# A feed-forward block in two stages: 2x2 block products for the up projection, a trip through DRAM, and a down projection by four feature tiles

## The chip, the cores and the metric

One core of one Trainium2 chip runs the whole program. Times are microseconds of device time for one execution. Of the kernel before, three runs are given; the profile is of one further execution.

## The reference

Two layers of a hybrid backbone over 1024 latent tokens of width 1024, with 256 context tokens beside them in layer 0 (layer 1 computes the latent tokens alone). Each layer is a modulated RMSNorm, an input projection into three head groups (latent attention, a state space scan, windowed attention), an output projection with a gated residual, and then the part that changes:

```python
def conv_glu(h, w_up, conv_w, conv_b, w_down):
    val, gate = jnp.split(h @ w_up, 2, axis=-1)
    return (jax.nn.silu(dwconv(gate, conv_w, conv_b)) * val) @ w_down

h2 = modulate(rms_norm(x, p['norm2_g']), sh2, sc2)
x = x + g2 * conv_glu(h2, p['ffn_w_up'], p['ffn_conv_w'], p['ffn_conv_b'], p['ffn_w_down'])
```

`w_up` is 1024 x 5632, so 2816 hidden features (22 tiles of 128) for the gate and 2816 for the value; `w_down` is 2816 x 1024. The convolution runs along the tokens with three taps. The modulation vectors (`mod`, twelve pieces of 512 columns per layer, each for the latent and for the context conditioning) are the product of a conditioning vector with `w_mod`.

## The kernel before

Activations lie with features on the partitions and tokens in the free dimension: eight tiles of 128 features for `x`, in token chunks of 512, 512 and (layer 0) 256. Every matrix product keeps nearly full fp32 precision by splitting both operands into a high and a low part and adding three products, so that one 128 x 128 weight tile against 512 tokens is three matmuls (`PASSES`, helper `mm` at L142):

```python
PASSES = ((0, 0), (0, 1), (1, 0))
```

A weight tile is fetched by SP (L410), cast to its high part by ACT (L420), and its low part is the difference on DVE (L421).

`ffn` walks over the 22 feature tiles. For each it makes the gate projection (24 matmuls per chunk of 512), whose result goes through bias and middle tap on ACT (L500), the two outer taps on DVE (L496) and SiLU on ACT (L508); then the value projection, whose result is multiplied into the gate by DVE (L1522), cast by ACT (L1523) and split by POOL (L1524). After every second tile, `do_down` adds what these two features give to all eight output tiles: six matmuls per output and chunk, and one DVE instruction that adds the result to `x` (L1501). So PE always has up and down products of the same stretch to run, and `x` stays in the on-chip memory.

The input of the block is prepared by `Norm`: DVE multiplies `x` by the inverse norm (L1911, L1917), ACT and DVE make high and low parts. `Norm` starts when the last outputs of the output projection `w_out` are there; the first gate product waits for it.

Modulation vectors are made by `mods_v` without PE's help: SP fetches two rows of blocks of `w_mod` (L344, 512 KB), DVE multiplies and adds (L349, L351), PE transposes 128 columns at a time into the tile `pt` (L147), and DVE sums (L358). It is a background generator: the program's planner gives it a turn after every `gap` of planned PE time. Six pieces of layer 0 run in the input projection of layer 0 (`early`), two more and all twelve of layer 1 in the FFN of layer 0.

SP issues all large transfers from one queue, in program order; each may wait for a semaphore, and what stands behind it waits with it.

## Time and profile before

| what | value |
|---|---|
| runs | 3346.91 us median of 3 (3344.35 to 3354.57) |
| the profiled execution | 3349.32 us, of which the span 3347.6 us |
| mean granted clock of TensorE | 0.967 of full speed |
| busy share: PE, DVE, ACT, POOL | 94%, 58%, 32%, 24% |
| FFN of layer 0 in the trace | about 902 to 1850 us |
| FFN of layer 1 in the trace | about 2588 to 3307 us |

The page and the views count an engine as busy while an instruction of it executes; matmuls are pipelined, so that their single durations overlap, and the rate of a stretch is its length over its count. The granted clock is the share of TensorE's full speed (2.4 GHz) that was allowed in a stretch; the lower level is 1.2 GHz.

### The profile page before, as it was taken

The page shows a single profiled execution, that of the slowest core. Times are in us where ns is not written, and L with a number is a line of the kernel's source. Part 1 is how long each engine was busy: PE and PEld are TensorE (multiplying, and loading weights), DVE is VectorE, ACT ScalarE, POOL GpSimd, SP SyncE. Part 2 cuts the span into 40 slices and gives each one's busy share as a digit, 9 for nine tenths or more (in the row PEclk, how much of TensorE's full clock was granted, in tenths as well). Part 3 has the DMA queues.
Part 4 walks back from the last instruction along what each step waited for, and adds up shares of the span by engine and source line. Part 5 has one row for each costly group of instructions (what it writes and reads, how often), then busy time and mean ns, then how long its engine had stood idle before and what let it go on. Part 6 is the DMA issues. An engine that isn't in the chain of part 4 may idle for free.

```text
span 3347.6 us, 40209 instructions
## 1 busy us (share of the span) xinstructions
PE 3160.3 (94%) x15857; PEld 2496.6 (75%) x15857; DVE 1948.8 (58%) x2912; ACT 1068.7 (32%) x1764; POOL 804.2 (24%) x518
## 2 busy tenths in 40 slices
PE   6999879989989999999999999879999999999998
PEld 4888645546878888888888788645558788888887
DVE  5966877664485565656544734886653544444444
ACT  5344543443331111111112533533342312212222
POOL 2115533452220000000001304553451200101102
PEclk9999879999999999999999999988999999999999
DMA  8765663103132222222111444843121111111111
GB/s 262 215 182 165 220 223 88 41 5 114 38 95 76 65 87 70 82 70 82 57 39 29 143 138 139 264 144 94 41 73 41 57 51 51 45 44 57 46 49 64
DMA packets 311550, 321.64 MB, mean 96 GB/s; under 512 B 34835, under 2 KB 250532, under 8 KB 311361
## 3 DMA queue, kind: packets, MB, share of 16 engines
q1 hardware_dynamic: 310396, 318.83, 31.1%
q8 instruction: 125, 2.05, 0.3%
q0 software_dynamic: 704, 0.14, 0.2%
q14 instruction: 65, 0.52, 0.0%
q10 hardware_dynamic: 260, 0.10, 0.0%
HBM read 249.09 MB, written 68.62 MB: 95 GB/s over the span
## 4 chain that ended last, share of the span: by engine, by line
PE 72%; DVE 8%; DMA 2%; issue 1%; ACT 1%; POOL 1%; SPq 0%; DVEq 0%; POOLq 0%; ACTq 0%
PE p L142 58%; PE s L142 5%; PE py L142 4%; DVE mx L1291 1%; DMA wm<-in_w_mod_dram 1%; DVE wm L351 1%; PE pm L142 1%; PE pn L142 1%; PE pd L142 1%; DVE acc L1326 1%; PE sb L142 0%; DMA ab<-acsd 0%; DVE sh L725 0%; DVE smx L1045 0%; PE pst L142 0%
## 5 line engine op out<-in xcount | busy, mean ns | idle before, releaser
L142 PE MATMUL p<-hhi,wh 128*128 128x512 f32 (+1 forms) x2552 | 943.8, 372 | 12.5 <-DVE ft L496 5.2
L142 PE MATMUL p<-hlo,wh 128*128 128x512 f32 (+2 forms) x2552 | 940.8, 369 | 7.4 <-POOL hlo L1920 6.6
L142 PE MATMUL p<-hhi,wl 128*128 128x512 f32 (+1 forms) x2504 | 923.6, 369 | 5.8 <-DVE wl L421 3.5
L142 PEld LDWEIGHTS p<-hhi,wh 128*128 128x128 f32 x2552 | 485.3, 190 | 95.6 <-issue 7.0
L142 PEld LDWEIGHTS p<-hlo,wh 128*128 128x128 f32 (+1 forms) x2552 | 483.2, 189 | 87.2 <-POOL hlo L1920 8.3
L142 PEld LDWEIGHTS p<-hhi,wl 128*128 128x128 f32 x2504 | 476.3, 190 | 87.2 <-DVE wl L421 5.6
L1524 POOL TENSOR_TENSOR gl<-ft,gh 128x512 fp32r<-128x512 f32 (+1 forms) x110 | 152.7, 1390 | 1404.6 <-ACT gh L1523 1404.6
L1501 DVE SCALAR_TENSOR_TENSOR x<-p,modT,x 128x512 f32<-128x512 f32 (+1 forms) x480 | 327.2, 695 | 240.2 <-PE p L142 239.8
L420 ACT CAST wh<-w 128x1024 fp32r<-128x1024 f32 (+2 forms) x188 | 193.2, 1040 | 751.4 <-PE p L142 706.3
L142 PE MATMUL p<-gh,wh 128*128 128x512 f32 (+1 forms) x880 | 325.7, 370 | 0.4 <-DVE x L1501 0.4
L142 PE MATMUL p<-gl,wh 128*128 128x512 f32 (+1 forms) x880 | 324.7, 369 | 0.0
L142 PE MATMUL p<-gh,wl 128*128 128x512 f32 (+1 forms) x880 | 323.9, 368 | 0.0
L421 DVE TENSOR_TENSOR wl<-w,wh 128x1024 fp32r<-128x1024 f32 (+1 forms) x181 | 224.9, 1252 | 146.5 <-ACT wh L420 145.3
L496 DVE SCALAR_TENSOR_TENSOR ft<-p,prm,ft 128x511 f32<-128x511 f32 (+2 forms) x264 | 157.8, 613 | 176.2 <-ACT ft L500 173.5
L351 DVE SCALAR_TENSOR_TENSOR wm<-wm,mstat,wm 128x512 f32<-128x512 f32 x280 | 202.6, 767 | 60.0 <-DMA wm<-in_w_mod_dram 59.9
L1375 ACT ACTIVATE P<-s 128x512 f32<-128x512 f32 x240 | 142.5, 598 | 247.0 <-PE s L142 240.8
L1522 DVE TENSOR_TENSOR ft<-ft,p 128x512 f32<-128x512 f32 (+1 forms) x110 | 69.4, 633 | 257.9 <-PE p L142 256.7
L1382 POOL TENSOR_TENSOR acc<-acc,P 128x1024 f32<-128x1024 f32 x69 | 169.5, 2456 | 185.1 <-ACT P L1375 162.3
L142 PEld LDWEIGHTS p<-gh,wh 128*128 128x128 f32 x880 | 165.9, 189 | 29.2 <-DVE x L1501 0.9
L142 PEld LDWEIGHTS p<-gh,wl 128*128 128x128 f32 x880 | 165.6, 188 | 28.2
L142 PEld LDWEIGHTS p<-gl,wh 128*128 128x128 f32 x880 | 166.0, 189 | 27.5 <-issue 0.2
L142 PE MATMUL py<-P,vt 128*64 128x512 f32 (+3 forms) x744 | 172.3, 578 | 0.0
(354 smaller groups left out, 4486.2 us busy)
## 6 DMA issues: line engine op xcount, KB each, us to landing
wm<-in_w_mod_dram SPq DMA_DIRECT2D x96, 512.0 KB
w<-in_ffn_w_up_dram SPq DMA_DIRECT2D x88, 512.0 KB
w<-in_ffn_w_down_dram SPq DMA_DIRECT2D x44, 512.0 KB
w<-in_w_in_dram SPq DMA_DIRECT2D x30, 512.0 KB
ab<-acsd SPq DMA_DIRECT2D x36, 384.0 KB
...
```

What stands on the lines that cost most here:

```text
L142: self.nc.tensor.matmul(out=out, lhsT=lhsT, rhs=rhs, start=start, stop=stop)
L351: nc.vector.scalar_tensor_tensor(out=acc[:, v, :], in0=w[:, i, :], scalar=c, in1=acc[:, v, :], op0=ALU.mult, op1=ALU.add)
L420: nc.scalar.copy(h, w)
L421: (nc.gpsimd if pool else nc.vector).tensor_sub(lo, w, h)
L496: nc.vector.scalar_tensor_tensor(out=dst[:, d0:d1], in0=src, scalar=w, in1=dst[:, d0:d1], op0=ALU.mult, op1=ALU.add)
L1291: nc.vector.tensor_reduce(out=m[:, j, s:s + 1], in_=p, axis=AXX, op=ALU.max)
L1326: nc.vector.reciprocal(rc, pd)
L1375: nc.scalar.activation(P[:, q * 512:(q + 1) * 512], s, AF.Exp, scale=sc)
L1382: (nc.vector if kt in ((2, 4, 6, 8) if self.scan else (4, 7)) else nc.gpsimd).tensor_add(acc, acc, P)
L1501: self.nc.vector.scalar_tensor_tensor(out=t[:, s:e], in0=p[:, 0:e - s], scalar=self.mcol(l, v, m)[:, o:o + 1], in1=t[:, s:e], op0=ALU.mult ...
L1522: nc.vector.tensor_mul(t[:, s:e], t[:, s:e], p[:, 0:e - s])
L1524: nc.gpsimd.tensor_sub(gl[:, s:e], t[:, s:e], gh[:, s:e])
```

## The change

The block becomes two stages per layer.

**Up.** A unit is a pair of neighbouring feature tiles of the gate or of the value (22 units: gate pair, value pair, gate pair, and so on). For the 1024 latent tokens a unit is a 2 x 2 block product: the weights in two column tiles by two halves of the depth (four 128-deep tiles each), the tokens in two halves of 512. Of the eight block products only seven are computed (with sums and differences of blocks ahead of and behind them). `UpNorm` makes the token blocks: 11, 12, 21, 22 as `Norm` did, then T1 to T4 as differences, in place in `x`, each split again into high and low parts. `up_weights` makes the weight blocks 11, 12, 22 and S1 to S4, and `wblock` splits each. `step` runs one product of 12 matmuls, and the results are added up in two tiles `cm` of the on-chip memory by DVE and ACT. `wrap` then does the convolution and SiLU, or the multiplication by the value, and writes the finished tile to DRAM (`gd`). Unit 0 is computed plainly; context tokens keep all their products.

**Down.** When all tiles are in DRAM, `gload` reads them back, ACT and DVE split them, and `down` takes four feature tiles at a time (two in the last group): 12 matmuls per output and chunk, then one addition to `x`. As `x` was used up for the blocks, `w_out` now also writes it to DRAM (`xsp`) and the down stage reads it again.

**Modulation.** Two pieces of layer 0 move from its FFN to `early` (eight pieces there, gap 3.0 for 4.0). Layer 1's twelve pieces move to the down stage of layer 0; eight of them are made for the latent conditioning alone (`nv`), and all must be done before the last group.

```diff
+GROUPS = [range(i, min(i + 4, NF)) for i in range(0, NF, 4)]
...
-    def mods_v(self, l, ns, wtile, gap, atile=None):
+    def mods_v(self, l, ns, wtile, gap, atile=None, nv=lambda n: 2):
...
-                    for v in range(2):
+                    for v in range(nv(n)):
...
+    def wblock(self, raw):
+
+        self.nblock += 1
+        t = self.W.tile([128, 2, *raw.shape[1:]], F32R, tag=("whi", "wlo")[self.nblock % 2], name=self.nm("wb"))
+        self.nc.scalar.copy(t[:, 0], raw)
+        self.nc.vector.tensor_sub(t[:, 1], raw, t[:, 0])
+        return t
...
+    def up_names(self, l, u):
+        return ("11", "12", "21", "22") if u == 0 else ("11", "12", "22", *(("21",) if l == 0 else ()), "S1", "S2", "S4", "S3")
...
+                if name == "S1":
+                    nc.vector.tensor_sub(a11, a11, a21)
+                    nc.vector.tensor_add(a21, a21, a22)
+                    raw = a21
+                elif name == "S2":
+                    nc.vector.tensor_sub(a22, a22, a11)
+                    raw = a22
+                elif name == "S4":
+                    nc.vector.tensor_sub(a12, a12, a22)
+                    raw = a12
+                else:
+                    raw = {"11": lambda: a11, "12": lambda: a12, "21": lambda: a21, "22": lambda: a22, "S3": lambda: a11}[name]()
+                w = self.wblock(raw)
+                if name == ("12" if u == 0 else "S4"):
+                    load(u + 1, 0)
+                if name == ("22" if u == 0 else "S3"):
+                    load(u + 1, 1)
...
+        def done(o, p, s, e):
+            self.resid(res[o], p, s, e, l, 2, o)
+            nc.sync.dma_start(out=self.spill[o][:, s:e], in_=res[o][:, s:e])
+            norm.feed(o, s, e)
...
+        def product(w, blk, psum, start, stop=True):
+            for k in range(4):
+                for i, (a, b) in enumerate(PASSES):
+                    self.mm(out=psum, lhsT=w[:, a, k, :], rhs=blk[k][b], start=(start and k == 0 and i == 0), stop=(stop and k == 3 and i == 2),
+                            skip_group_check=True)
+            self.tick()
...
+        def put(U_, j, half, p):
+            d = U_.cm[j][:, half * 512:(half + 1) * 512]
+            if (j, half) in U_.set:
+                nc.vector.tensor_add(d, d, p)
+            else:
+                nc.scalar.copy(d, p)
+            U_.set.add((j, half))
...
+            if s == "1":
+                U_.X = self.f("X")
+                product(weight(u, "11"), B["11"], U_.X, True)
+                put(U_, 0, 0, U_.X)
+            elif s == "2":
+                Y = self.f("Y")
+                product(weight(u, "12"), B["21"], Y, True)
+                put(U_, 0, 0, Y)
+            elif s == "4":
+                V = self.f("V")
+                product(weight(u, "22"), B["T4"], V, True)
+                put(U_, 1, 0, V)
+            elif s == "5":
+                U_.Z = self.f("Z")
+                product(weight(u, "S1"), B["T1"], U_.Z, True)
+                put(U_, 1, 1, U_.Z)
+            elif s == "6":
+                product(weight(u, "S2"), B["T2"], U_.X, False)
+                put(U_, 0, 1, U_.X)
+            elif s == "3":
+                product(weight(u, "S4"), B["22"], U_.Z, False)
+                put(U_, 0, 1, U_.Z)
+            elif s == "7":
+                product(weight(u, "S3"), B["T3"], U_.X, False)
+                out7(U_)
...
+        def wrap(u):
+
+            U_ = units.pop(u)
+            for j in range(2):
+                f = u // 2 * 2 + j
+                srcs = [(0, SEQ, U_.cm[j][:, LAT])] + ([(SEQ, NT, U_.pc[:, 256 * j:256 * j + 256])] if c else [])
+                if u % 2 == 0:
+                    t = gate[f] = self.u(name="ft")
+                    w0, w1, w2, b = conv_of(f)
+                    for s, e, p in srcs:
+                        nc.scalar.activation(t[:, s:e], p, AF.Identity, bias=b, scale=w1)
+                        for d0, d1, q, w in ((s + 1, e, p[:, 0:e - s - 1], w0), (s, e - 1, p[:, 1:e - s], w2)):
+                            nc.vector.scalar_tensor_tensor(out=t[:, d0:d1], in0=q, scalar=w, in1=t[:, d0:d1], op0=ALU.mult, op1=ALU.add)
+                    nc.scalar.activation(t[:, 0:n], t[:, 0:n], AF.Silu)
+                else:
+                    t = gate.pop(f)
+                    for s, e, p in srcs:
+                        nc.vector.tensor_mul(t[:, s:e], t[:, s:e], p)
+                    nc.sync.dma_start(out=self.gd[f][:, 0:n], in_=t[:, 0:n])
...
+        ps = plain(*chunks[0])
+        step(1, "1")
+        step(1, "2")
+        norm.need(chunks[1])
+        for j in range(2):
+            cv[j](ps[j], *chunks[0])
+        ps = plain(*chunks[1])
+        norm.built("T1")
+        if c:
+            norm.need(chunks[2])
+        for j in range(2):
+            cv[j](ps[j], *chunks[1])
+        if c:
+            for s in ("c11", "c12", "c21", "c22"):
+                step(0, s)
+        norm.built("T2")
+        norm.built("T3")
+        if c:
+            for j in range(2):
+                cv[j](units[0].pc[:, 256 * j:256 * j + 256], *chunks[2])
+            for s in ("c11", "c12", "c22", "c21"):
+                step(1, s)
+        norm.built("T4")
+        del units[0]
+        for s in ("5", "3", "6", "7", "4"):
+            step(1, s)
+        wrap(1)
+        for u in range(2, NF):
+            for s in ("1", "c11", "2", "c12", "4", "c22", "c21", "5", "6", "3", "7") if c else ("1", "2", "4", "5", "6", "3", "7"):
+                step(u, s)
+            wrap(u)
...
+        def gload(fs):
+            for f in fs:
+                t, h, lo = self.u(name="gr"), self.u(F32R, name="gh"), self.u(F32R, name="gl")
+                nc.sync.dma_start(out=t[:, 0:n], in_=self.gd[f][:, 0:n])
+                g[f] = h, lo
+                for s, e in chunks:
+                    nc.scalar.copy(h[:, s:e], t[:, s:e])
+                    nc.vector.tensor_sub(lo[:, s:e], t[:, s:e], h[:, s:e])
...
+        gload(GROUPS[0])
+        for o in range(KT):
+            t = self.X.tile([128, NT], F32, tag="x", name=self.nm("x"))
+            nc.sync.dma_start(out=t[:, 0:n], in_=self.spill[o][:, 0:n])
+            x.append(t)
+        start()
+        for i, fs in enumerate(GROUPS[:-1]):
+            for q in range(4):
+                ws = self.wnext(2, ahead=6)
+                for o in (2 * q, 2 * q + 1):
+                    for s, e in chunks:
+                        down(fs, ws, o, s, e)
+                if q == 0:
+                    gload(GROUPS[i + 1])
+            for f in fs:
+                del g[f]
+        before_last()
+        fs = GROUPS[-1]
+        ws = self.wnext(4, ahead=5)
+        for s, e in chunks:
+            for o in range(KT):
+                down(fs, [ws[o // 2]], o, s, e)
+                feed(o, s, e)
...
-            self.X = PoolTags(p, {"x": 8, "ft": 1, "wm": 2, "pn": 1} if l == 0 else {"x": 8, "ft": 1, "wm": 2})
+            self.X = PoolTags(p, {"x": 8, "ft": 1, "wm": 2, "pn": 1} if l == 0 else {"x": 9, "wm": 2})
...
-                        yield from self.mods_v(0, range(4, 10), wt, 4.0)
+                        yield from self.mods_v(0, range(4, 12), wt, 3.0)
...
+                    yield from self.mods_v(l + 1, range(12), xw, 4.6, xa, lambda n: 2 if n < 4 else 1)
...
+    def parts(self, name, k, raw, hi=None, lo=None):
+        nc = self.E.nc
+        if hi is None:
+            t = self.slot(name, k)
+            hi, lo = t[:, 0:512], t[:, 512:1024]
+        nc.scalar.copy(hi, raw)
+        nc.vector.tensor_sub(lo, raw, hi)
+        self.blk[name][k] = hi, lo
...
+            r = self.x[f][:, s:e]
+            hf, k = f // 4 + 1, f % 4
+            nc.vector.tensor_mul(r, r, pn[:, 0:e - s])
+            nc.scalar.activation(r, r, AF.Identity, bias=b[v][:, f:f + 1], scale=a[:, v, f:f + 1])
+            if v:
+                self.parts(f"c{hf}", k, r, self.slot(f"{hf}1", k)[:, SEQ:NT], self.slot("T1" if hf == 1 else "22", k)[:, SEQ:NT])
+            else:
+                self.parts(f"{hf}{1 if s == 0 else 2}", k, r)
...
+    def built(self, name):
+        nc = self.E.nc
+        for k in range(4):
+            t, u = self.x[k], self.x[4 + k]
+            c0, c1 = slice(*CHUNKS[0]), slice(*CHUNKS[1])
+            if name == "T1":
+                nc.vector.tensor_sub(t[:, c0], t[:, c1], t[:, c0])
+                self.parts(name, k, t[:, c0])
+            elif name == "T2":
+                nc.vector.tensor_sub(t[:, c1], u[:, c1], t[:, c1])
+                nc.vector.tensor_sub(u[:, c1], u[:, c1], t[:, c0])
+                self.parts(name, k, u[:, c1])
+            elif name == "T3":
+                self.parts(name, k, t[:, c1])
+            else:
+                nc.vector.tensor_sub(u[:, c0], u[:, c0], u[:, c1])
+                self.parts(name, k, u[:, c0])
```

`Norm` now feeds the blocks through `UpNorm.apply`. Lines of the changed program are shifted: its matmul helper is L143, its low parts of weights L437, of token blocks L2153.

**PE, a stretch of the up projection of layer 1.** Before, one output of 512 tokens is 24 matmuls into `p`:

```order
L142 MATMUL p_24083<-hhi_20121,wh_23945 128x512 [waits Activation_49]
L142 MATMUL p_24083<-hlo_20122,wh_23945 128x512
L142 MATMUL p_24083<-hhi_20121,wl_23946 128x512 [waits DVE_49]
L142 MATMUL p_24083<-hhi_20127,wh_23945 128x512
L142 MATMUL p_24083<-hlo_20128,wh_23945 128x512
L142 MATMUL p_24083<-hhi_20127,wl_23946 128x512
L142 MATMUL p_24083<-hhi_20134,wh_23945 128x512
```

Now a product is 12 matmuls, and some products go on in a bank that already holds another one (here `Z` of S1, `X` of S2 over `X`, then `Z` of S4 over `Z`):

```order
L143 MATMUL Z_20796<-hb_20437,wb_20695 128x512 [waits DVE_49,Activation_49]
L143 MATMUL Z_20796<-hb_20437,wb_20695 128x512 x2
L143 MATMUL Z_20796<-hb_20441,wb_20695 128x512 x3
L143 MATMUL Z_20796<-hb_20445,wb_20695 128x512 x3
L143 MATMUL Z_20796<-hb_20449,wb_20695 128x512 x3
L143 MATMUL X_20740<-hb_20466,wb_20712 128x512 [waits Activation_49]
L143 MATMUL X_20740<-hb_20466,wb_20712 128x512
L143 MATMUL X_20740<-hb_20466,wb_20712 128x512 [waits DVE_49]
L143 MATMUL X_20740<-hb_20471,wb_20712 128x512 x3
L143 MATMUL X_20740<-hb_20476,wb_20712 128x512 x3
L143 MATMUL X_20740<-hb_20481,wb_20712 128x512 x3
L143 MATMUL Z_20796<-hb_20360,wb_20742 128x512 [waits Activation_49]
```

Between the two visits to `Z` there is one product into `X`; `Z` is read out in between.

**SP, the end of the up projection of layer 0.** Before, the queue of the FFN holds weights (`w`) and pieces of `w_mod` (`wm`) in turn:

```order
L410 DMA w_12482<-in_ffn_w_up_dram 128x8x128 [waits DMAHW5_49,DVE_49]
L344 DMA wm_12426<-in_w_mod_dram 128x2x512 [waits DMAHW7_49,DVE_49]
L344 DMA wm_12535<-in_w_mod_dram 128x2x512 [waits DMAHW1_49,DVE_49]
L410 DMA w_12706<-in_ffn_w_up_dram 128x8x128 [waits DMAHW6_49,DVE_49]
L344 DMA wm_12643<-in_w_mod_dram 128x2x512 [waits DMAHW2_49,DVE_49]
L410 DMA w_12712<-in_ffn_w_up_dram 128x8x128 [waits DMAHW0_49,DVE_49]
```

Now the reload of `x`, the finished tiles (`gd<-ft`), the tiles read back (`gr`), down weights and pieces of `w_mod` stand in one line. The first group of the down stage needs four `gr`: the second, third and fourth are here, and the last two `x` wait for PE's last product:

```order
L1761 DMA x_11833<-xsp 128x1280 [waits DMAHW0_49,PE_49]
L1741 DMA gr_11791<-gd 128x1280 [waits DMAHW1_49,Pool_49]
L1761 DMA x_11835<-xsp 128x1280 [waits PE_49]
L1686 DMA gd<-ft_11581 128x1280 [waits DMAHW3_49,DVE_49]
L347 DMA wm_11867<-in_w_mod_dram 128x2x512 [waits DMAHW4_49,PE_49]
L613 DMA w_12103<-in_ffn_w_down_dram 128x4x256 [waits DMAHW6_49,DMAHW5_49,DVE_49]
L1686 DMA gd<-ft_11589 128x1280 [waits DVE_49]
L1741 DMA gr_11801<-gd 128x1280 [waits DMAHW7_49]
L347 DMA wm_11909<-in_w_mod_dram 128x2x512 [waits DMAHW0_49]
L347 DMA wm_11997<-in_w_mod_dram 128x2x512 [waits DMAHW4_49,DMAHW1_49,DVE_49]
L1741 DMA gr_11811<-gd 128x1280 [waits DMAHW2_49]
```

The fourth `gr` stands behind a `wm` that waits for DVE.

**DVE, the start of the FFN of layer 1.** Before, normalised tokens (`nt`) and their low parts (`hlo`):

```order
L1917 TENSOR_TENSOR nt_20310<-x_19604,pn_20254 128x512 [waits Pool_49]
L1911 SCALAR_TENSOR_TENSOR nt_20315<-x_19737,a_20118,pn_20254 128x512
L1917 TENSOR_TENSOR nt_20319<-x_19803,pn_20254 128x512
L1914 SCALAR_TENSOR_TENSOR hlo_20122<-nt_20306,modT_8021,hhi_20121 128x512 [waits Activation_49]
L1914 SCALAR_TENSOR_TENSOR hlo_20135<-nt_20315,modT_8021,hhi_20134 128x512 [waits Activation_49]
L1911 SCALAR_TENSOR_TENSOR nt_20328<-x_19869,a_20118,pn_20254 128x512
L1917 TENSOR_TENSOR nt_20332<-x_19935,pn_20254 128x512 [waits DVE_49]
L1911 SCALAR_TENSOR_TENSOR nt_20337<-x_19972,a_20118,pn_20254 128x512 [waits DVE_49]
L1917 TENSOR_TENSOR nt_20341<-x_20003,pn_20254 128x512 [waits Pool_49]
```

Now, further on in the same place, sums into `cm`, low parts of weights (`wb`) and of token blocks (`hb`), and differences of weights:

```order
L1610 TENSOR_TENSOR cm_20296<-cm_20296,X_20298 128x512 [waits PE_49,Activation_49]
L437 TENSOR_TENSOR wb_20516<-w_20303,wb_20516 128x512 [waits Activation_49]
L586 TENSOR_TENSOR w_20323<-w_20323 128x512 [waits DVE_49]
L2153 TENSOR_TENSOR hb_20497<-x_19887,hb_20497 128x512 [waits Activation_49]
L1685 TENSOR_TENSOR ft_20200<-ft_20200,cm_20296 128x1024 [waits DVE_49,Activation_49]
L589 TENSOR_TENSOR w_20323<-w_20323,w_20303 128x512 [waits DVE_49]
L2153 TENSOR_TENSOR hb_20501<-x_19955,hb_20501 128x512 [waits Activation_49]
L592 TENSOR_TENSOR w_20303<-w_20303,w_20323 128x512 [waits DVE_49]
L437 TENSOR_TENSOR wb_20567<-w_20323,wb_20567 128x512 [waits Activation_49]
L2153 TENSOR_TENSOR hb_20505<-x_19992,hb_20505 128x512 [waits Activation_49]
L2153 TENSOR_TENSOR hb_20487<-x_19614,hb_20487 128x512 [waits DMAHW2_49,Activation_49]
L2153 TENSOR_TENSOR hb_20509<-x_20024,hb_20509 128x512 [waits Activation_49]
```

The last four of the token blocks of T4 (`hb_20497` to `hb_20509`) stand among the work of unit 1; one row of T3 (`hb_20487`) also waits for a transfer.

## Rows read from the trace of the kernel before

**Rows 1.** The page of the profile: the span, busy time by engine, the chain's shares.

```profile
span 3347.6 us, 40209 instructions
PE 3160.3 (94%) x15857; PEld 2496.6 (75%) x15857; DVE 1948.8 (58%) x2912; ACT 1068.7 (32%) x1764; POOL 804.2 (24%) x518
...
PE 72%; DVE 8%; DMA 2%; issue 1%; ACT 1%; POOL 1%; SPq 0%; DVEq 0%; POOLq 0%; ACTq 0%
PE p L142 58%; PE s L142 5%; PE py L142 4%; DVE mx L1291 1%; DMA wm<-in_w_mod_dram 1%; DVE wm L351 1%; PE pm L142 1%; PE pn L142 1%; PE pd L142 1%; DVE acc L1326 1%; PE sb L142 0%; DMA ab<-acsd 0%; DVE sh L725 0%; DVE smx L1045 0%; PE pst L142 0%
```

**Rows 2.** Stretches: middle of the FFN in layer 0 and in layer 1, all engines.

```profile
core 0: us, PE busy (x) PEld busy (x) DVE busy (x) ACT busy (x) POOL busy (x), PEclk, DMA share, GB/s
1000.00:1600.00 600.00, 600.00 (x3166) 517.20 (x3165) 364.85 (x592) 113.53 (x155) 53.72 (x42) 1.00 0.25 75
2740.00:3140.00 400.00, 400.00 (x1766) 331.20 (x1766) 172.27 (x247) 81.22 (x96) 37.19 (x24) 1.00 0.16 48
```

**Rows 3.** Groups by line, 2740 to 3140 us: out<-in, shapes, count, busy us, mean ns, idle before.

```profile
L1501 DVE SCALAR_TENSOR_TENSOR x<-p,modT,x 128x512 f32<-128x512 f32 x103 | 77.2, 749 | 47.5 <-PE p L142 47.5
...
L421 DVE TENSOR_TENSOR wl<-w,wh 128x1024 fp32r<-128x1024 f32 x36 | 43.5, 1223 | 48.0 <-ACT wh L420 48.0
...
L496 DVE SCALAR_TENSOR_TENSOR ft<-p,prm,ft 128x511 f32<-128x511 f32 x48 | 35.9, 747 | 51.4 <-ACT ft L500 50.8
L500 ACT ACTIVATE ft<-p,prm 128x512 f32<-128x512 f32 x24 | 18.7, 779 | 49.9 <-PE p L142 49.9
L1522 DVE TENSOR_TENSOR ft<-ft,p 128x512 f32<-128x512 f32 x24 | 16.5, 688 | 81.5 <-PE p L142 81.5
L1523 ACT CAST gh<-ft 128x512 fp32r<-128x512 f32 x24 | 14.8, 617 | 38.5 <-DVE ft L1522 38.5
L508 ACT ACTIVATE ft<-ft 128x1024 f32<-128x1024 f32 x12 | 12.7, 1061 | 39.6 <-DVE ft L496 39.6
```

**Rows 4.** The input projection of layer 0, 86 to 201 us: the stretch, then two of its groups.

```profile
86.00:201.00 115.00, 109.74 (x613) 95.55 (x613) 108.03 (x181) 43.33 (x68) 13.31 (x15) 0.99 0.74 224
...
L351 DVE SCALAR_TENSOR_TENSOR wm<-wm,mstat,wm 128x512 f32<-128x512 f32 x84 | 59.3, 746 | 1.2 <-DMA wm<-in_w_mod_dram 1.2
...
L349 DVE TENSOR_SCALAR wm<-wm,mstat 128x512 f32<-128x512 f32 x12 | 5.3, 478 | 4.5 <-DMA wm<-in_w_mod_dram 4.5
L358 DVE TENSOR_REDUCE modT<-pt 128x4 f32<-128x512 f32 x8 | 5.2, 678 | 0.0
```

**Rows 5.** Timeline of that stage's end: start us, us, engine, line, [idle before].

```profile
205.25 1.66 DVE L496 SCALAR_TENSOR_TENSOR xbc<-p,prm,xbc 128x511 f32<-128x511 f32 x3 [3.27 <-ACT xbc L500]
...
207.75 1.29 DVE L358 TENSOR_REDUCE modT<-pt 128x4 f32<-128x512 f32 x2 [0.71 <-PE pt L147]
...
207.11 2.04 PE L147 MATMUL pt<-ident,wm 128*128 128x128 f32 x16
```

**Rows 6.** Stretches: the first 100 us of the FFN in layer 0.

```profile
900.00:1000.00 100.00, 86.47 (x420) 72.07 (x419) 77.15 (x126) 38.49 (x63) 25.68 (x18) 0.93 0.30 91
940.00:960.00 20.00, 13.34 (x84) 12.22 (x82) 15.24 (x26) 8.89 (x12) 4.03 (x4) 0.83 0.20 57
```

**Rows 7.** Stretches: the first 120 us of the FFN in layer 1.

```profile
2580.00:2700.00 120.00, 114.22 (x483) 92.41 (x482) 60.11 (x86) 42.66 (x57) 27.41 (x17) 0.96 0.16 49
2600.00:2620.00 20.00, 16.50 (x55) 12.75 (x53) 8.09 (x10) 5.15 (x9) 7.10 (x4) 0.74 0.36 106
```

**Rows 8.** Waits of PE, 900 to 1000 us: in total, times, longest (us).

```profile
PE p L142 <- DVE ft L496: 5.2, 2, 4.6
PE p L142 <- POOL hlo L1920: 3.4, 1, 3.4
```

**Rows 9.** Stretches inside the reload of x before the output projection of layer 0.

```profile
774.00:777.50 3.50, 3.50 (x22) 1.69 (x20) 0.00 (x0) 2.04 (x3) 2.73 (x2) 1.00 1.02 423
777.50:781.00 3.50, 0.63 (x6) 0.14 (x2) 2.76 (x3) 0.97 (x1) 0.00 (x0) 0.96 1.07 346
```

More of the change, by code (lines that the diff above doesn't have):

```diff
@@ L141, in mm @@
         self.t += c
-        self.nc.tensor.matmul(out=out, lhsT=lhsT, rhs=rhs, start=start, stop=stop)
+        self.nc.tensor.matmul(out=out, lhsT=lhsT, rhs=rhs, start=start, stop=stop, **kw)
     def tr(self, out, in_):
@@ L558, in ffn_weights @@
[L558 to L560 removed]
+        return out + self.up_weights(l) + self.down_weights(l)
     def evac(self, t, M):
@@ new lines, in ffn, with unit, weight @@
+        B = norm.blk
+        gate, units = {}, {}
+        class Unit:
+            pass
+        def unit(u):
+            if u not in units:
+                U_ = units[u] = Unit()
+                U_.names, U_.w, U_.set, U_.cm, U_.pc = list(self.up_names(l, u)), {}, set(), None, None
+            return units[u]
+        def weight(u, name):
+            U_ = unit(u)
+            while name not in U_.w:
+                U_.w[U_.names.pop(0)] = self.wnext(ahead=6)
+            return U_.w[name]
@@ new lines, in out7, with step @@
+        def out7(U_):
+            if {(1, 0), (1, 1)} <= U_.set:
+                d = U_.cm[1][:, LAT].rearrange("p (a n) -> p a n", a=2)
+                nc.vector.tensor_add(d, d, U_.X.unsqueeze(1).to_broadcast([128, 2, 512]))
+            else:
+                for half in range(2):
+                    put(U_, 1, half, U_.X)
+        def step(u, s):
+            U_ = unit(u)
+            if U_.cm is None and u:
+                if u % 2:
+                    U_.cm = [self.X.tile([128, SEQ], F32, tag="wm", name=self.nm("cm")) for _ in range(2)]
+                else:
+                    U_.cm = [self.X.tile([128, NT], F32, tag="x", name=self.nm("cm")) for _ in range(2)]
+            if s == "1":
[24 more added lines that the diff above has]
+            else:
+                j, k = int(s[1]) - 1, int(s[2]) - 1
+                if U_.pc is None:
+                    U_.pc = self.b("pc")
+                first = (j, "c") not in U_.set
+                U_.set.add((j, "c"))
+                product(weight(u, s[1:]), B["c1" if k == 0 else "c2"], U_.pc[:, 256 * j:256 * j + 256], first, not first)
@@ new lines, in plain @@
+        def plain(s, e):
+            ps = []
+            for j in range(2):
+                p = self.f("p")
+                for k in range(2):
+                    product(weight(0, f"{j + 1}{k + 1}"), B[f"{k + 1}{1 if s == 0 else 2}"], p, k == 0, k == 1)
+                ps.append(p)
+            return ps
+        norm.need(chunks[0])
+        for f in range(2):
+            gate[f] = self.u(name="ft")
+        cv = [self.conv(gate[f], *conv_of(f)) for f in range(2)]
+        ps = plain(*chunks[0])
```

185 lines of the change are left out of this document (98 added, 87 removed).

## Prediction

> **What bounds the kernel now.** I read the page first: PE is busy for 94% of the span, DVE for 58%, and 72% of the chain that ended last is PE's, 58% in products into `p` alone [rows 1]. Then the stretches by engine. In the middle of both FFNs PE is never idle and its granted clock is 1.00, while DVE is busy 61% of the time in layer 0 and 43% in layer 1 [rows 2]. So there the time is the number of matmuls times their spacing, and nothing else counts until another engine falls behind. In layer 1 all matmuls have 512 columns: 400 us over 1766 is **0.2265 us each**. In layer 0 the same division gives 0.1895 for a mix of two 512s to one 256, so a 256 costs 3 x 0.1895 - 2 x 0.2265 = 0.116 us. Two kinds of places are not like that: the start of each FFN, where PE waits for the normalised tokens and runs at a lower clock [rows 6 to 8], and the input projection of layer 0, where DVE is the busy one (108.0 of 115 us) and the DMA share is 0.74 [rows 4]. The change takes matmuls out of the first kind of stretch and puts waits into the second.
>
> **The change, part by part.** The sum goes against the profiled execution, 3349.3 us; the median is 2.4 us below it.
>
> *Matmuls.* A pair of tiles took 96 matmuls of 512 columns and now takes 84, in 21 of 22 units per layer: 2 x 21 x 12 = 504 fewer, x 0.2265 = **-114 us**. All stood in stretches without idle PE. Context products (1056 of 256 columns) and down products are as many as before. Making eight pieces of layer 1's modulation for one conditioning saves 32 transposes; sixteen take 2.04 us [rows 5]: **-4**.
>
> One rule would make this term smaller. Rows 2 give 0.2265 us. The Trainium skill ("TensorE: Matmul & The Clock Gate", section "Back-to-back issue gap") states about 131 ns for a sustained stream of 512-column matmuls with their weight loads; by that the term would be 504 x 0.131 = -66 and the forecast some 48 us later, no change. No stretch of this trace runs at that spacing, so the trace decides, and the rule has no chance of its own.
>
> *Early modulation.* Two more pieces in a stage where DVE is full. One piece is 14 multiply-adds of 0.746, 2 first products of 0.478 and 2 sums of 0.678 [rows 4]: 12.8 us, back to back nearer 11.7; two are 23.4. DVE has 7 us idle in the stage [rows 4] and 3.3 + 0.7 just behind it [rows 5]. If all of that takes work, 12 are left; if little does, 24; if the stage ends on PE and transfers instead, 6. I take **+14** (6 to 24). What this hides in the FFN of layer 0 is worth nothing: it ran beside a full PE.
>
> *Start of layer 0's FFN.* From the first `x` times the inverse norm to the last low part of T4, DVE now has 122 instructions: 79 of 512 elements at 0.688 [rows 3], the others shorter, about 74 us. PE has 15 products of 12 x 0.2265 and 8 of 12 x 0.116 in that time, 52 us. The difference of 22 less some 2 us of output projection that is left is the stall. Before, the first 100 us lost 13.5 us of idling and 0.07 x 86.5 = 6 of clock [rows 6], 19 in all, the single longest wait being 4.6 [rows 8]. **+2** (0 to 10).
>
> *Start of layer 1's FFN.* The same count: 112 DVE instructions, 93 of them of 512 elements, 75 us; PE has 15 products, 41 us, and some 8 us of output projection. The stall is about 26; before it was 5.8 idle and 0.04 x 114 = 4.6 of clock [rows 7]. **+15** (8 to 22). ACT, with 0.62 per cast and 0.78 per scaled copy [rows 3], is nearly as full and could add a little; that is in the range.
>
> *Up to down, layer 0.* The first output needs four tiles read back, since PE takes them in order. On SP's queue, behind the last product, stand two reloads of `x`, two finished tiles, three tiles to read, three pieces of `w_mod` and one down weight: 7 x 0.655 + 4 x 0.524 = 6.7 MB. The reload of `x` before the output projection reached 423 GB/s, and 346 in its last slice [rows 9]; the input projection's mix moved 224 at a share of 0.74 [rows 4], 303 at a full one. So 16 to 22 us, plus the multiplication that the finished tiles wait for (three DVE rows, 2 to 3 us) and the split of the last tile (ACT 0.62, DVE 0.69), less the 2 us of matmuls that can run: **+19** (10 to 30). The Trainium skill ("DMA: Bandwidth & Descriptors", section "Where 436 GB/s comes from") holds that about 358 GB/s of HBM binds such transfers; by it the 6.7 MB take 18.7 us. Rows 9 show 423, above that limit, so the trace allows less, but only with long pieces.
>
> *Up to down, layer 1.* Five of the eight reloads go earlier, no `w_mod` stands in the line, tiles are 0.524 MB: two reloads, one finished tile and one tile to read remain at the end, and the fourth tile is there some 15 us after the last product: **+14** (5 to 20).
>
> *Layer 0's down stage with modulation.* A group of four tiles is 8 outputs of 24 x 0.2265 + 12 x 0.116 = 6.8 us, 55 us of PE; in it DVE has 24 residuals (0.749 and shorter), 8 low parts of weights and 12 of tiles (0.69 and shorter), some 28 us. The first pieces (both conditionings) are 16 multiply-adds, 11 to 12 us, in every 4 turns of 4.6 us: DVE is slightly over. **+5** (0 to 20). Once one conditioning is left it fits.
>
> *Steady units.* PE needs 84 x 0.2265 = 19.0 us in layer 1 and 24.6 in layer 0; DVE has 12 to 16 of it (seven low parts of weights, four or five block differences, six sums of 0.69, two taps or a product). PE stays the bound. The read-out of `Z` has one product, 2.7 us, to happen in. **+4** (0 to 30).
>
> *Clock.* At the start of layer 1's FFN 3.5 us of idling went with 16.5 us at a clock of 0.74, 4.3 us lost [rows 7]; at 940 to 960 the loss was 2.3 [rows 6]. Two new long stalls: **+7** (4 to 9).
>
> Sum: -114 - 4 + 14 + 2 + 15 + 19 + 14 + 5 + 4 + 7 = -38; 3349.3 - 38 = 3311, and by the median about **3309 us**. The new writes of `x` in the output projections (8 x 0.655 + 8 x 0.524 = 9.4 MB) I cost at nothing: PE's products there cover them; without that cover, a weight load queued on SP behind a write that waits for its residual would show as a wait of PE for `w`.
>
> **Rivals.** A measurement of this kernel can tell about 0.3% (10 us) from no change.
>
> *The block products wait for their own read-out (slower).* Each unit goes back to a bank three times, and each time ACT or DVE must have read it. These instructions stand in line behind casts and differences that wait for transfers. If a unit loses 2 us, 40 units cost 80 and the time is 3387; from 1.2 us a unit the change is slower than before. For it: DVE is in order, and its rows now wait for transfers and ACT. Against it: DVE has a quarter or more of each unit free, and before, read-outs of this kind cost PE 5.2 us in two waits at a start [rows 8] and none in the middle [rows 2]. Chance 0.18.
>
> *The stalls cost twice what I take (no change).* Starts, transitions and clock are +57 in my sum; with 33 more, near their upper ends, the time is about 3342. That needs a low transfer rate and ACT behind as well as DVE. Chance 0.12.
>
> *The covers hold.* If the reloads and tiles are there when the last product ends and DVE is ahead at the starts, only some 25 us are given back: 3349 - 118 + 25 = 3256. The queue order of SP speaks against it: the last two reloads wait for the last product. Chance 0.13.
>
> *The forecast*: 10 to 80 us faster, chance 0.57; its own range is 3270 to 3337.
>
> **How the numbers follow.** Faster by over 0.3% is the forecast and the covers: 0.70; within: 0.12; slower: 0.18. The range of 8 in 10 runs from 3255 (the covers hold) to 3385 (nearly 2 us a unit).
>
> **What would show it.** Right: a middle of the up stages at clock 1.00 without idle PE and 0.2265 us per matmul; one stall of 15 to 25 us of PE between up and down in each layer, released by tiles read back; FFN starts with 20 to 26 us lost, released by DVE; an input projection of layer 0 that ends 6 to 24 us later. Wrong: PE waits in every unit; a stage of down products where DVE is full; or no stall at the change of stage.

## The result and the profile after

The changed kernel takes 3298.69 us (median of 4, 3295.10 to 3301.97) against 3348.87 us (median of 4) of the kernel before on the same chip: **0.9853 of the time, 95% interval 0.9838 to 0.9867**, 50 us less. 3309 was forecast.

The page of the changed kernel, to set beside [rows 1]:

```profile
span 3300.3 us, 40044 instructions
PE 3067.8 (93%) x15321; PEld 2408.6 (73%) x15321; DVE 2145.1 (65%) x3172; ACT 1275.9 (39%) x2203; POOL 614.6 (19%) x382
```

PE is busy for 92 us less, and the span is 47 us shorter. DVE has 196 us more to do. There are 536 fewer matmuls, the 504 block products and 32 transposes of the forecast. The stretches of the changed kernel tell where the rest of the gain went; the first two rows are the middles of the two up stages, then the two starts, the two changes of stage, and the down stage of layer 0:

```profile
core 0: us, PE busy (x) PEld busy (x) DVE busy (x) ACT busy (x) POOL busy (x), PEclk, DMA share, GB/s
1000.00:1400.00 400.00, 400.00 (x2129) 346.34 (x2128) 240.77 (x337) 158.25 (x240) 0.00 (x0) 1.00 0.21 69
2700.00:3000.00 300.00, 300.00 (x1325) 248.43 (x1324) 209.81 (x267) 134.03 (x204) 0.00 (x0) 1.00 0.26 84
900.00:1000.00 100.00, 85.92 (x433) 70.09 (x432) 80.98 (x147) 59.33 (x106) 0.00 (x0) 0.97 0.14 44
2590.00:2700.00 110.00, 92.71 (x380) 72.45 (x379) 83.16 (x130) 54.27 (x88) 0.00 (x0) 0.92 0.19 58
1480.00:1520.00 40.00, 23.16 (x88) 16.62 (x87) 26.37 (x43) 11.23 (x22) 0.00 (x0) 0.74 0.89 327
3020.00:3060.00 40.00, 33.25 (x130) 25.63 (x130) 23.11 (x33) 13.20 (x24) 0.00 (x0) 0.87 0.77 288
1540.00:1800.00 260.00, 259.60 (x1384) 224.43 (x1383) 191.16 (x325) 38.82 (x71) 0.00 (x0) 1.00 0.48 149
```

The middles are as full as before [rows 2]: no idle PE, clock 1.00, 1325 matmuls in 300 us of layer 1, which is 0.2264 us each. At the starts, layer 0 loses 14.1 us of idling and 2.6 of clock where it lost 19 [rows 6]; layer 1 loses 17.3 and 7.4 where it lost 10 [rows 7]. The changes of stage are new: 16.8 us of idling with 23.2 us busy at a clock of 0.74 (6 more lost, together some 23), and 6.8 with 33.2 at 0.87 (together 11). The down stage with the modulation behind it runs as full as a middle.

What PE waits for at the change of stage of layer 0 (waits of PE, 1470 to 1560 us: in total, times, longest):

```profile
PE p L143 <- ACT gh L1744: 15.5, 3, 7.0
PE p L143 <- DVE gl L1745: 1.3, 2, 1.1
```

and why the tiles are late, in SP's line of transfers there (start, us, engine, line, transfer); the last product of the up stage ends at about 1491.3:

```profile
1489.73 0.38 SPq L1741 DMA_DIRECT2D gr<-gd  x1
1490.66 0.32 SPq L1761 DMA_DIRECT2D x<-xsp  x1
1491.07 0.39 SPq L1686 DMA_DIRECT2D gd<-ft  x1
1491.55 0.99 SPq L347 DMA_DIRECT2D wm<-in_w_mod_dram  x1
1495.05 0.38 SPq L613 DMA_DIRECT2D w<-in_ffn_w_down_dram  x1
1496.18 0.34 SPq L1686 DMA_DIRECT2D gd<-ft  x1
1496.57 0.68 SPq L1741 DMA_DIRECT2D gr<-gd  x1
1497.30 7.74 SPq L347 DMA_DIRECT2D wm<-in_w_mod_dram  x2
1505.08 0.47 SPq L1741 DMA_DIRECT2D gr<-gd  x1
```

The last row is the fourth tile of the first group. It was issued at 1505.08, behind two `wm`, whose issue took from 1497.30 on. What SP's queue waits for meanwhile (1497 to 1505.1 us: in total, times, longest) is for the greater part an earlier transfer of `wm`, and then DVE:

```profile
SPq L347 <- DMA wm<-in_w_mod_dram: 4.6, 1, 4.6
SPq L347 <- DVE wm L354: 2.2, 1, 2.2
```

ACT split the fourth tile from here:

```profile
1511.28 1.45 ACT L1744 CAST gh<-gr 128x512 fp32r<-128x512 f32 x3 [2.92 <-DMA gr<-gd]
```

That is 20 us after the last product. PE had waited for the second and the third tile too: 6.1 us, 7.0 and 2.4 for the three in turn.

In the input projection of layer 0, PE now waits at its transposes for DVE's multiply-adds of the modulation pieces (waits of PE, 100 to 230 us; before, there is no such wait from 86 to 260 us):

```profile
PE pt L148 <- DVE wm L354: 13.9, 3, 6.7
```

To cut the span into pieces I use two events that both kernels have: the first norm statistics ahead of each FFN (`pn`), and the first attention scores of layer 1 (`s`). Each line is from an answer of its own, and its last two times are the first and the last start. Before, and after:

```profile
L142 PE MATMUL pn<-ones,acc x16: 166/250/250, 883.4 to 912.3; 128*128 128x1 f32 x16
L142 PE MATMUL s<-qh,kh x120: 392/403/800, 2183.8 to 2496.3; 97*128 97x512 f32 x120
L142 PE MATMUL pn<-ones,acc x16: 164/250/352, 2581.0 to 2613.5; 128*128 128x1 f32 x16
```

```profile
L143 PE MATMUL pn<-ones,acc x16: 164/250/250, 902.9 to 927.8; 128*128 128x1 f32 x16
L143 PE MATMUL s<-qh,kh x120: 390/400/796, 2166.4 to 2478.2; 97*128 97x512 f32 x120
L143 PE MATMUL pn<-ones,acc x16: 164/250/250, 2562.9 to 2591.7; 128*128 128x1 f32 x16
```

| from, to | before | after | difference |
|---|---|---|---|
| start to `pn` of layer 0 | 883.4 | 902.9 | +19.5 |
| `pn` of layer 0 to `s` of layer 1 | 1300.4 | 1263.5 | -36.9 |
| `s` of layer 1 to `pn` of layer 1 | 397.2 | 396.5 | -0.7 |
| `pn` of layer 1 to the end | 766.6 | 737.4 | -29.2 |

### The profile page after: what moved, and what is told of

Read it like the earlier page. It is cut to its first block, busy times and chain, and to the rows that moved or that the text cites. A ratio compares the mean times of both kernels' runs of the same rounds, so it can differ in the third digit from the quotient of the medians.

```text
span 3300.3 us, 40044 instructions
## 1 busy us (share of the span) xinstructions
PE 3067.8 (93%) x15321; PEld 2408.6 (73%) x15321; DVE 2145.1 (65%) x3172; ACT 1275.9 (39%) x2203; POOL 614.6 (19%) x382
## 4 chain that ended last, share of the span: by engine, by line
PE 76%; DVE 14%; DMA 5%; issue 2%; ACT 2%; POOL 1%; SPq 0%; DVEq 0%; ACTq 0%; POOLq 0%
PE p L143 33%; PE X L143 10%; PE Z L143 7%; PE s L143 6%; PE py L143 5%; PE pc L143 4%; PE V L143 3%; PE Y L143 3%; DVE wm L354 2%; DVE mx L1362 1%; DMA gr<-gd 1%; PE pm L143 1%; DVE hb L2153 1%; PE pn L143 1%; PE pst L143 1%
## 5 line engine op out<-in xcount | busy, mean ns | idle before, releaser
L143 PE MATMUL p<-gh,wb 128*128 128x512 f32 (+1 forms) x1760 | 508.2, 372 | 20.5 <-ACT gh L1744 20.5
L437 DVE TENSOR_TENSOR wb<-w,wb 128x512 fp32r<-128x512 f32 x411 | 281.2, 689 | 260.6 <-ACT wb L436 256.4
L143 PEld LDWEIGHTS p<-gh,wb 128*128 128x128 f32 x1760 | 322.4, 190 | 79.5 <-ACT gh L1744 23.8
L143 PE MATMUL X<-hb,wb 128*128 128x512 f32 x1512 | 360.4, 391 | 9.5 <-ACT hb L2152 4.6
L143 PEld LDWEIGHTS X<-hb,wb 128*128 128x128 f32 x1512 | 284.8, 189 | 70.9 <-ACT hb L2152 5.3
L143 PE MATMUL p<-gl,wb 128*128 128x512 f32 (+1 forms) x880 | 327.2, 372 | 2.6 <-DVE gl L1745 2.6
L143 PE MATMUL p<-hhi,wh 128*128 128x512 f32 (+1 forms) x792 | 292.6, 377 | 5.4 <-ACT z L648 3.1
L143 PE MATMUL p<-hlo,wh 128*128 128x512 f32 (+3 forms) x792 | 290.9, 368 | 1.9 <-DVE hlo L2123 1.0
L143 PE MATMUL p<-hhi,wl 128*128 128x512 f32 (+1 forms) x744 | 273.3, 367 | 3.6 <-DVE wl L424 3.1
L143 PE MATMUL Z<-hb,wb 128*128 128x512 f32 x1008 | 245.8, 393 | 8.7 <-ACT wb L436 4.4
L143 PEld LDWEIGHTS Z<-hb,wb 128*128 128x128 f32 x1008 | 189.1, 189 | 49.4 <-ACT wb L436 4.6
L143 PEld LDWEIGHTS p<-gl,wb 128*128 128x128 f32 x880 | 167.1, 190 | 32.8 <-DVE gl L1745 5.1
L143 PEld LDWEIGHTS p<-hhi,wh 128*128 128x128 f32 x792 | 152.1, 193 | 32.0 <-ACT z L648 4.0
L143 PE MATMUL py<-P,vt 128*64 128x512 f32 (+3 forms) x744 | 174.3, 584 | 0.0
L143 PEld LDWEIGHTS p<-hlo,wh 128*128 128x128 f32 (+1 forms) x792 | 150.2, 190 | 25.4 <-DVE hlo L2123 1.7
L143 PEld LDWEIGHTS p<-hhi,wl 128*128 128x128 f32 x744 | 143.0, 192 | 28.4 <-DVE wl L424 4.4
```

Source lines behind the costliest of these rows:

```text
L143: self.nc.tensor.matmul(out=out, lhsT=lhsT, rhs=rhs, start=start, stop=stop, **kw)
L437: self.nc.vector.tensor_sub(t[:, 1], raw, t[:, 0])
```

## The experiments

Ratios are to the kernel before on the same chip; a difference in us is the difference of two such ratios times 3347 us. Each ratio is known to about 0.0015, so a difference of two is good to some 7 us. In the code, "..." stands for lines that are not shown.

**Eight block products in the same two stages (e1).** The theory was that a matmul is worth its spacing, and the loss lies outside the units.

```diff
-        return ("11", "12", "21", "22") if u == 0 else ("11", "12", "22", *(("21",) if l == 0 else ()), "S1", "S2", "S4", "S3")
+        return ("11", "12", "21", "22") if u >= 0 else ("11", "12", "22", *(("21",) if l == 0 else ()), "S1", "S2", "S4", "S3")
...
-            for s in ("1", "c11", "2", "c12", "4", "c22", "c21", "5", "6", "3", "7") if c else ("1", "2", "4", "5", "6", "3", "7"):
-                step(u, s)
+            eight(u)
...
```

> The two stages stay, but every unit computes all eight block products (each output of 512 tokens is 24 matmuls again), with no differences of token or weight blocks. Theory: a matmul is worth its spacing, so 504 more of 0.2265 us are +114 us; the work of DVE that goes (28 instructions per layer ahead of the units) shortens the two starts by 10 to 30, and the blocks leave the on-chip memory sooner, so that the reload of x may leave the transitions, up to 10 more. So 75 to 105 us longer than the changed kernel, about 3375 to 3405. Rival (sums and read-outs of the block products hold PE up inside the units, so that seven products gain less than their count): 50 us longer or less, and then idle PE in the middle of the changed kernel's units that is not there with eight.

Measured 1.0036 (1.0022 to 1.0050): 61 us longer than the changed kernel, between the two. Its stretches in the middle of the up stage of layer 0, then at the starts and at the changes of stage, layer 0 first and then layer 1 of each:

```profile
1000.00:1400.00 400.00, 400.00 (x2104) 345.82 (x2103) 115.64 (x152) 114.40 (x164) 0.00 (x0) 1.00 0.21 63
900.00:1000.00 100.00, 97.61 (x493) 81.66 (x492) 51.85 (x99) 50.51 (x88) 0.00 (x0) 0.98 0.18 56
2600.00:2700.00 100.00, 94.04 (x404) 75.36 (x403) 45.01 (x70) 43.67 (x69) 0.00 (x0) 0.98 0.23 71
1500.00:1540.00 40.00, 34.48 (x190) 29.36 (x188) 22.09 (x36) 15.22 (x27) 0.00 (x0) 0.97 0.50 169
3020.00:3060.00 40.00, 40.00 (x178) 33.14 (x177) 12.77 (x14) 12.98 (x19) 0.00 (x0) 1.00 0.31 104
```

PE was not idle in the middle of either kernel's units (in layer 1 the eight fill 300.00 of 300 us from 2700 on, with 1326 matmuls), so the rival's mechanism is out: 57 us per layer are saved there. But eight products lose only 4.4 us at the start of layer 0 and 7.9 in layer 1, some 7 at the first change of stage (5.5 idle, the clock at 0.97) and nothing at the second. The seven lose 16.7, 24.7, 23 and 11. The differences are 12, 17, 16 and 11, 56 us at four places; by the time itself 53 of the 114 us are given back. I had expected the token blocks to cost the changes of stage only 10 in all; that was the miss.

**The two moved pieces left out (e2).**

```diff
+            self.nc.vector.memset(self.modT[l], 0.0)
...
-                        yield from self.mods_v(0, range(4, 12), wt, 3.0)
+                        yield from self.mods_v(0, range(4, 10), wt, 3.0)
```

> The two pieces of layer 0's modulation (10 and 11) that were moved into its input projection are left out of the computation altogether (zeros in their place). Theory: that stage ends on DVE, which was full before, so the two pieces are on the path: 15 to 20 us shorter than the changed kernel, 3279 to 3284, and PE no longer waits 6 us twice for their sums. Rival (they lie beside PE's work and the later end has another cause): 5 us shorter or less.

Measured 0.9810 (0.9792 to 0.9828), 14 us shorter, just under what was expected; `pn` of layer 0 comes at 883.3, as in the kernel before. The pieces were on the path. With `pn` back at its old place, the new writes of `x` ahead of it show no cost.

**Tiles first at the change of stage (e3).** Nothing is moved but SP's order: `gload` is called within the last unit, and `issue_after` queues the rest behind its last transfer (pieces of `w_mod` and down weights in the same way, by lines that are not shown).

```diff
...
+                if u == NF - 1 and s == "5":
+                    behind = gload(GROUPS[0])
+            if u < NF - 1:
+                wrap(u)
+        with self.tc.issue_after(behind):
+            wrap(NF - 1)
...
-            nc.sync.dma_start(out=t[:, 0:n], in_=self.spill[o][:, 0:n])
+            with self.tc.issue_after(behind):
+                nc.sync.dma_start(out=t[:, 0:n], in_=self.spill[o][:, 0:n])
```

> Only the order on SP's queue at the change of stage: the four finished tiles of the first down group are asked for during the last unit, and the reloads of x, the last two finished tiles, later down weights and pieces of the modulation weights are queued behind them. Theory: PE waits there for the order of the queue, not for the amount of data: 33 us of idling and low clock in both layers shrink to under 10, so 20 to 30 us shorter than the changed kernel, about 3270 to 3278. Rival (the transfer rate bounds the stretch, and what is put back is waited for next, as x by the first residuals): the stall moves by some us into the down stage, 8 us shorter or less.

Measured 0.9810 (0.9796 to 0.9823), 14 us shorter: less than expected. The two changes of stage:

```profile
1480.00:1520.00 40.00, 33.21 (x164) 27.72 (x162) 28.32 (x47) 10.61 (x22) 0.00 (x0) 0.96 0.86 323
3005.00:3045.00 40.00, 40.00 (x178) 33.14 (x177) 27.45 (x39) 17.86 (x30) 0.00 (x0) 1.00 0.78 291
```

In layer 1 the stall is gone. In layer 0 it shrank from 16.8 to 6.8 in that stretch, and PE has a new wait (waits of PE, 1460 to 1560 us):

```profile
PE pt L149 <- DVE wm L359: 11.6, 3, 11.0
```

PE comes to the transposes of the first modulation piece, in its fixed order, before DVE has made the piece. So neither text was right in full: the order of the queue set the stall, and in layer 0 part of what the new order saved was lost at the next work in line.

**The same with the modulation started later (e5).** The edit of e3, and:

```diff
-                self.ffn(l, x, norm, nxt.feed, lambda: self.bg(mods(), 4.0), lambda: self.until(lambda: self.gated))
+                self.ffn(l, x, norm, nxt.feed, lambda: self.bg(mods(), 20.0), lambda: self.until(lambda: self.gated))
```

> The order of e3_tiles_first, and the modulation of layer 1 starts 20 instead of 4 planned us into the down stage. In e3 the stall between the stages went, but PE then waited 11 us in one place, at its transposes of a modulation piece that DVE had not made yet. Theory (that wait is the start of the pieces colliding with the tiles and residuals at the start of the stage): 8 to 12 us shorter than e3, about 22 to 28 shorter than the changed kernel. Rival (DVE cannot make the pieces at that rate whenever they start): the wait moves to a later transpose or to the end of the stage, within 4 us of e3.

Measured 0.9775 (0.9762 to 0.9789), 26 us shorter than the changed kernel. The wait for the pieces is 4.0 where it was 11.6:

```profile
PE pt L149 <- DVE wm L359: 4.0, 2, 3.7
```

**POOL makes the low parts of T1 to T4 (e4).**

```diff
-        nc.vector.tensor_sub(lo, raw, hi)
+        (nc.gpsimd if name[0] == "T" else nc.vector).tensor_sub(lo, raw, hi)
```

> The low parts of the token blocks T1 to T4 (16 subtractions of 512 per layer, 11 us of DVE) are made by POOL, which is idle in these stretches; POOL takes about 1.4 us for one. Theory (DVE sets the two starts): 8 to 18 us shorter, more in layer 1 than in layer 0. Rival (ACT's casts, or POOL itself at 1.4 us each, set them): within 4 us of the changed kernel.

Measured 0.9901 (0.9888 to 0.9915), **16 us longer**: both were wrong. Groups of DVE and of POOL in the start of layer 0 while POOL works (946 to 968 us):

```profile
L2153 DVE TENSOR_TENSOR hb<-x,hb 128x256 fp32r<-128x256 f32 x7 | 8.7, 1281 | 0.0
L2183 DVE TENSOR_TENSOR x<-x,x 128x512 f32<-128x512 f32 x4 | 5.8, 1498 | 0.0
L508 DVE SCALAR_TENSOR_TENSOR ft<-p,prm,ft 128x511 f32<-128x511 f32 x5 | 3.6, 740 | 0.0
...
L2153 POOL TENSOR_TENSOR hb<-x,hb 128x512 fp32r<-128x512 f32 x12 | 19.6, 1661 | 70.3 <-ACT hb L2152 70.3
```

and of the changed kernel at the same place (946 to 975 us):

```profile
L508 DVE SCALAR_TENSOR_TENSOR ft<-p,prm,ft 128x511 f32<-128x511 f32 x8 | 5.8, 741 | 0.0
L2153 DVE TENSOR_TENSOR hb<-x,hb 128x256 fp32r<-128x256 f32 x8 | 2.9, 417 | 0.0
L2183 DVE TENSOR_TENSOR x<-x,x 128x512 f32<-128x512 f32 x4 | 2.7, 683 | 0.0
```

POOL takes 1.66 us for one, and meanwhile DVE's subtractions of two operands in the on-chip memory take 1.28 us instead of 0.42 (256 elements) and 1.50 instead of 0.68 (512; the mean of one at 0.69 as POOL began and three at some 1.7). The instruction that reads one operand from the accumulators (L508, 0.74) is as fast as ever. So DVE got 32 instructions fewer and no less time (2150.5 us in all, where the changed kernel has 2145.1).

**Those low parts not made at all (e8).**

```diff
+        if name[0] == "T":
+            lo = hi
+        else:
+            nc.vector.tensor_sub(lo, raw, hi)
```

> The 16 low parts per layer of the token blocks T1 to T4 are not computed (the high part is read in their place, so the output is not the reference's); PE, ACT and the differences are as before. Theory (DVE sets the two starts): 11 us less of DVE in each, so 6 to 11 us shorter per layer, 12 to 22 in all. Rival (ACT's casts set them): within 5 us of the changed kernel.

Measured 0.9822 (0.9808 to 0.9835), 10 us shorter for 20 us less of DVE. The start of layer 0, and two pieces of it:

```profile
900.00:1000.00 100.00, 91.09 (x474) 76.31 (x473) 72.86 (x134) 59.96 (x109) 0.00 (x0) 0.97 0.15 49
935.00:945.00 10.00, 5.91 (x18) 3.59 (x17) 10.00 (x21) 10.00 (x19) 0.00 (x0) 0.83 0.00 0
945.00:955.00 10.00, 9.15 (x44) 7.39 (x44) 10.00 (x20) 10.00 (x23) 0.00 (x0) 1.00 0.00 1
```

From 935 to 955 ACT is as full as DVE (10.00 of 10 each). So it seems that the starts hang on both: taking 10 us of DVE's work out of each gives 5. No run takes work from ACT alone.

**The two pieces in the output projection of layer 0 (e6).**

```diff
...
+                def two():
+                    yield from self.mods_v(0, (10, 11), lambda shape: self.u(shape=shape, name="wm"), 7.0)
+                    self.gated = True
...
+                self.bg(two(), 30.0)
             self.w_out(l, Y, hl, finish, x, norm)
...
```

> The two pieces of layer 0's modulation go from the input projection to the output projection of layer 0, where DVE is busy about a third of the time. Theory: the input projection loses 15 to 20 us as when they were left out, and PE covers them in the output projection: 12 to 18 us shorter than the changed kernel. Rival (DVE's line delays the normalisation, or PE waits for the transposes there): less than 8 us shorter.

Measured 0.9810 (0.9794 to 0.9825), 14 us shorter, as when they were left out: there they cost nothing that can be told.

**Both together (e7).** The edits of e5 and of e6 in one kernel.

> e5 and e6 together. Theory (the two places are apart in time and add): the sum of the two gains, 34 to 46 us shorter than the changed kernel, about 3255. Rival (they meet in the start of the feed-forward block): less than 28 us shorter.

Measured 0.9734 (0.9720 to 0.9747): 3257.25 us, 40 shorter than the changed kernel; 26 and 14 add.

**Unit 1 with eight products, on top of both (e9).** The seven products begin at unit 2, which takes its product with T4 last; T2 to T4 are made later.

```diff
-        return ("11", "12", "21", "22") if u == 0 else ("11", "12", "22", *(("21",) if l == 0 else ()), "S1", "S2", "S4", "S3")
+        return ("11", "12", "21", "22") if u <= 1 else ("11", "12", "22", *(("21",) if l == 0 else ()), "S1", "S2", "S4", "S3")
...
-        step(1, "1")
-        step(1, "2")
+        eight(1, ((0, 0),))
...
+        eight(1, ((1, 0),))
+        eight(1, ((0, 1), (1, 1)))
...
```

> On top of e7_both, unit 1 (the first value pair) is computed with all eight block products as unit 0 is; seven products begin at unit 2, whose product with T4 comes last. Theory (at the starts PE lacks work that needs no differences): one more product (2.7 us) and four fewer differences and sums per layer, in exchange for up to 8 us more of cover while T1 to T4 are made: 4 to 14 us shorter than e7 in all. Rival (the token blocks T2 to T4 must now wait for the products of unit 1, so that the stall moves from unit 1 to unit 2): within 4 us of e7, or longer.

Measured 0.9692 (0.9679 to 0.9706): **3242.34 us**, 14 shorter than both together and the fastest here. The starts of the two layers:

```profile
900.00:1000.00 100.00, 93.41 (x481) 77.93 (x480) 75.27 (x134) 55.03 (x96) 0.00 (x0) 0.98 0.15 45
2520.00:2650.00 130.00, 120.59 (x503) 95.02 (x502) 96.00 (x152) 68.14 (x113) 0.00 (x0) 0.96 0.21 66
```

PE idles 6.6 and 9.4 us there, where in e7, on which this is built, it idles 14.5 and 19.5 (the rows of e7 stand with e10, below). That is what the theory expected: PE had lacked work that needs no differences. But the edit also takes 21 instructions (17 us) from DVE, and e8 gave 10 us for 20; no run tells the two causes apart.

**Eight products with the repairs of e7 (e10).** The edits of e1, e3, e5 and e6 in one kernel.

> e7_both with all eight block products in every unit and no differences. Theory: with the transitions repaired, what the seven products still give back is the two starts alone, 12 and 17 us by the changed kernel against the eight-product one; 114 less 29 is 85: 75 to 95 us longer than e7, 3332 to 3352. Rival (the transitions cost the block products as much as before): about 55 us longer.

Measured 0.9977 (0.9967 to 0.9987), 81 us longer than both together, as the theory had it. The two starts of e7, layer 0 first, and then those of e10:

```profile
883.00:1000.00 117.00, 102.54 (x523) 84.70 (x524) 90.00 (x164) 65.55 (x117) 0.00 (x0) 0.97 0.13 42
2530.00:2650.00 120.00, 100.46 (x400) 77.12 (x399) 87.13 (x142) 61.73 (x102) 0.00 (x0) 0.90 0.18 56
880.00:1000.00 120.00, 117.54 (x603) 99.24 (x604) 61.13 (x112) 57.90 (x99) 0.00 (x0) 0.99 0.18 54
2572.00:2692.00 120.00, 114.64 (x493) 91.69 (x492) 55.60 (x86) 52.77 (x84) 0.00 (x0) 0.99 0.25 77
```

With idling and clock the seven products lose 18 and 30 us there, the eight 4 and 7, which is 37 us more; the times put 33 of the 114 at it. At the changes of stage the eight lose no less than the seven: 6.7 us of idling from 1440 to 1600 in layer 0 for 5.5 from 1440 to 1560, and none in layer 1 for either. So with the changes of stage repaired, the seven products give back the starts alone.

## Why the prediction was right

The direction and the size held (50 us measured, 38 to 40 forecast), and so did the mechanism: matmuls are saved at their spacing, and more than half of that is lost again at the starts, at the changes of stage and in the input projection. Several terms were too large, and the errors went partly against each other. Of the signs that were to show it right, two held in one layer only: the stall between up and down was 16.8 us in layer 0 but 6.8 in layer 1, not 15 to 25 in each, and the starts lost 16.7 and 24.7, not 20 to 26.

*Matmuls, -114 and -4.* The middles run at the same spacing with as little idle PE; e10 against e7 shows 81 of the 114 as time, and the starts account for the rest. The 32 transposes were not tried by themselves. By the Trainium skill's 131 ns ("TensorE: Matmul & The Clock Gate", section "Back-to-back issue gap") it would have been 66 before any loss; the middle rows show 226 ns after the change as before it.

*Early modulation, +14.* 14 when left out, 14 when moved elsewhere, each good to some 7 us. By `pn` the profiled execution shows 19.5, and it is no outlier: in six profiled executions with the two pieces in this stage `pn` comes at 897.0 to 902.9, in five without them at 877.6 to 883.3. So the term is 14 to 20, within its range.

*Starts, +2 and +15.* Measured -2 and +14, by idling and clock. That layer 1 came out is in part luck: the idling that the count of DVE instructions gave was too large in both (20 and 26 us counted; 14.1 and, with the waits ahead of 2590 us, 19.5 measured), and the clock, which had a term of its own, made up for it. DVE set most of the waits (8.9 of 14.0 us in layer 0, 13.5 of 19.5 in layer 1), ACT the others, and e8 points to ACT as a second bound, which I had only put into the range.

*Changes of stage, +19 and +14, with +7 of clock.* 23 and 11 with the clock in, 34 where these terms gave 40. In layer 0 the sum was right in mechanism and size: the fourth tile came 20 us after the last product, by the queue that was written down, and the transfers ahead of it filled that time (DMA share 0.94 to 1.05 in each 4 us from 1488 to 1508). The wait of `wm` for DVE that stands in the listing was the smaller part, 2.2 us. In layer 1 the fourth tile was put at some 15 us after the last product; ACT split it from 3040.57, 9 us after the end at 3031.8, so this term was too large. The data moved at up to 414 GB/s in layer 0:

```profile
1500.00:1504.00 4.00, 0.60 (x2) 0.00 (x0) 1.85 (x5) 0.00 (x0) 0.00 (x0) 0.50 1.05 414
```

That is above the 358 GB/s of the Trainium skill ("DMA: Bandwidth & Descriptors", section "Where 436 GB/s comes from"), so with this one core at work its limit does not hold in a piece of 4 us.

*Modulation in the down stage, +5, and steady units, +4.* Both zero, apart from 0.4 us of waiting. The rival of the read-outs fell with the latter: there is no wait in the middle rows. The new writes of `x`, put at nothing, show no cost: `pn` of e2 is at its old place in layer 0, and from `s` to `pn` layer 1 takes 0.7 us less than before.

What is left: with the 19.5 us of the profiled execution the pieces sum to -52, and its span says -47. The forecast had no term for the handover from layer 0 to layer 1, which before and after is:

```profile
1798.00:1978.00 180.00, 175.41 (x904) 146.54 (x903) 99.93 (x160) 83.81 (x136) 37.65 (x30) 1.00 0.35 104
1780.00:1960.00 180.00, 172.13 (x871) 143.46 (x870) 98.18 (x154) 78.50 (x129) 35.26 (x27) 0.98 0.34 103
```

PE idles 7.9 us where it idled 4.6, and the clock is 0.98 where it was 1.00, 3.4 us more: some 7 together, which closes the sum to 2 us. The longest new waits of PE there are for DVE (2.7 us for `accx`, 2.4 for `wl`).
